# A transformer pair in split fp32: the split weights' slots are shifted against the moving operands

## The chip, the core and the metric

The kernel runs on one core of a Trainium2 chip. The metric is the device time of one execution in microseconds. Three executions of the kernel before took 3043.42, 3047.98 and 3048.37 us; the median is 3047.98 us.

## What is computed

Two layers of one block on 512 tokens of width 1024, then one pass of a second block. Every product with a weight matrix is what matters here:

```python
proj = x @ w_in                                   # 1024 x 2336, twice
h = layer_norm(ALPHA * x + heads @ w_o, g, b)     # attention of three kinds before it
ffn = (silu(h @ w_gate) * (h @ w_up)) @ w_down    # inner width 2816
# second block, once
h  = h  + 0.5 * g1  * swiglu(modulate(h,  ...), w_ffn1_in, w_ffn1_out)
hc = hc + 0.5 * g1c * swiglu(modulate(hc, ...), w_ffn1_in, w_ffn1_out)   # 256 context tokens
q, k, v, rg, cv, ga, gb = split(modulate(h, ...) @ w_in)                 # retention, convolution, gates
h  = h + g2 * ((sigmoid(ga) * y_ret + sigmoid(gb) * y_conv) @ w_out)
h  = h + 0.5 * g3 * swiglu(modulate(h, ...), w_ffn2_in, w_ffn2_out)
out = rmsnorm(h, final_norm)
```

## The kernel before

Activations are held transposed: a tile has 128 features on the partitions and 512 tokens along the row (256 for the context). A weight chunk of 128 output features is one tile of 128 x 1024 fp32, eight slices of 128 columns, one for each 128 input features.

Products are made in three parts. A value is held as a rounded part `hi` (type fp32r) and the rest `lo`. `split` (L106) makes them: ScalarE copies the fp32 tile to `hi` (L108), VectorE subtracts (L109). `mm3` (L139) then issues three matmuls into one PSUM tile: `hi` weights with `hi` data (L141), `hi` weights with `lo` data (L142), `lo` weights with `hi` data (L143). `chunk` (L145) runs `mm3` over the slices. So each matmul has its own load of 128 weight columns, and the data stream past them: 512 columns in the rows named `mm`, 256 in the rows named `gc` and `dc` and in the halves.

`wload` (L111) brings one chunk: a DMA from SyncE's queue to a slot of the pool `wraw` (three slots of 4096 bytes a partition), then `split` into a `hi` and a `lo` slot. These come from the pool `whl`, three slots each, and while a pool `whx` is held (`hold`, L127, two slots each, in three stretches: from each layer's `w_o` to the end of its feed-forward part, and from `w_co` to the end of the kernel) from five in turn. In `vproj` (L1068) the roles are changed: the tokens are the stationary operand and the split weights of `w_v` move.

The order of work is the program's order. Each engine runs its own queue; the tile framework puts in the semaphores, and the scheduling of loads follows from the three raw slots and the three or five split slots.

Where tiles lie: pools are stacked from the left end of a partition in the order in which they are opened, those with `side="right"` from the right end. A tile takes its row's bytes, rounded up to 32. From the left come a reserved stretch, `const` (identity, `ones`, three columns `col128`, `col256`, `col1024`, the pair `blk`, the table `vec`, some small tables), `wraw`, `whl`, `small`, `tmp`, `xp` (the sixteen x tiles of 2048 bytes) and the pools of each stage. From the right come `top` with the tile `pad` of 96 bytes, then the accumulators, the context's tiles and `whx`. Adding up these sizes, the start of every `hi` and `lo` slot, of every x tile, hidden tile, head tile and context tile leaves the same remainder, 384, when it is divided by 512; in the retention stage the tiles of the pool `ret` leave 0, weights and data alike. The slice k of a chunk starts 512 bytes times k further on, so that every weight slice and the data that move past it start at the same remainder. The one exception is `w_kr` (L636), whose slices have 64 columns: every second one starts 256 bytes off.

Of the kernel before, what the change touches and what calls it, by code (L numbers as in the profile page):

```python
# [9 lines left out]
F32 = mybir.dt.float32  # L10
F32R = mybir.dt.float32r
# [51 lines left out]
class Kern:  # L63
    def __init__(self, ctx, tc, a, o):
        self.ctx, self.tc, self.nc, self.a, self.o = ctx, tc, tc.nc, a, o
        pool = lambda name, bufs, **kw: ctx.enter_context(tc.tile_pool(reuse_waits=RW, name=name, bufs=bufs, **kw))
        self.const = pool("const", 1)

        self.nc.vector.memset(pool("top", 1, side="right").tile([128, 24], F32, name="pad"), 0.0)
        self.wraw = pool("wraw", 3)  # L70
        self.whl = pool("whl", 3)
        self.small = pool("small", 2)
        self.tmp = pool("tmp", 2)
        self.xp = pool("xp", 1)
        self.dram = pool("scratch", 1, space=DRAM)
        self.ps_mm = pool("ps_mm", 3, space=PSUM)
        self.ps_s = pool("ps_s", 2, space=PSUM)
        self.ps_t = pool("ps_t", 2, space=PSUM)
        self.ps_o = pool("ps_o", 1, space=PSUM)
        nc = self.nc  # L80
        c = self.const
        self.ident = c.tile([128, 128], F32, name="ident")
        make_identity(nc, self.ident)
        self.ones = c.tile([128, 128], F32, name="ones")
        nc.vector.memset(self.ones, 1.0 / 128)
        self.col = {}
        self.pre = {}
        self.whx = None
        self.turn = 0
        self.nlo = 0  # L90
        for n in (128, 256, 1024):
            t = c.tile([128, 1], F32, name=f"col{n}")
            nc.vector.memset(t, 1.0 / n)
            self.col[n] = t
        self.blk = c.tile([128, 2], F32, name="blk")
        nc.vector.memset(self.blk, 0.0)
        nc.vector.memset(self.blk[0:64, 0:1], 1.0 / 64)
        nc.vector.memset(self.blk[64:128, 1:2], 1.0 / 64)
        self.vec = c.tile([128, NVEC], F32, name="vec")
# [11 lines left out]
    def wload(self, src, key=None):  # L111
        if key in self.pre:
            return self.pre.pop(key)
        n = src.shape[-1]
        raw = self.wraw.tile([128, 1024], F32, tag="raw", name="raw")[:, :n]
        self.nc.sync.dma_start(out=raw, in_=src)
        p = self.whl
        if self.whx is not None:
            if self.turn % (3 + self.nx) >= 3:
                p = self.whx  # L120
            self.turn += 1
        hi = p.tile([128, 1024], F32R, tag="hi", name="whi")[:, :n]
        lo = p.tile([128, 1024], F32R, tag="lo", name="wlo")[:, :n]
        self.split(raw, hi, lo)
        return hi, lo

# [1368 lines left out]
```

## Time and profile before

| what | value |
|---|---|
| runs | 3043.42, 3047.98, 3048.37 us (median 3047.98) |
| profiled execution, its own time | 3048.77 us |
| span of that execution, first to last instruction | 3047.0 us |
| mean granted TensorE clock | 0.996 of full speed |
| TensorE busy / weight loads busy | 3000.2 us (98%) / 2562.3 us (84%) |
| VectorE, ScalarE, GpSimd busy | 1883.5, 1138.7, 141.0 us |

The profile tells for each engine what it ran and what ended its idle time. TensorE's matmuls are pipelined: a row shows one from its start to the arrival of its last result, which overlaps the next one's, so the pace is read from start to start and not from the durations. PEld is the load of weights, which runs beside the matmul before.

### The profile page before, as it was taken

Reading aid. Unit: us, or ns where it says so; the run is one execution under the profiler, and the core shown is the slowest. Engines: PE = TensorE matmul, PEld = TensorE weight load, DVE = VectorE, ACT = ScalarE, POOL = GpSimd, SP = SyncE. Lnnn points to the kernel's source line nnn. Section 1 sums busy time; section 2 is a strip of 40 time slices with the busy share of each in tenths; the row PEclk is TensorE's granted clock in tenths of the full one; section 3 lists DMA queues with packets and bytes.
Section 4 is the critical chain, followed back from the end, with each engine's and each line's share of the span. In section 5 each row is a group of like instructions: output and inputs, shape, how many; then the busy total and the mean of one; then the engine's idle time right before and its main releaser. Section 6 shows DMA issues by size and latency. Waiting matters only on the chain.

```text
span 3047.0 us, 40882 instructions
## 1 busy us (share of the span) xinstructions
PE 3000.2 (98%) x15961; PEld 2562.3 (84%) x15961; DVE 1883.5 (62%) x3649; ACT 1138.7 (37%) x1876; POOL 141.0 (5%) x261
## 2 busy tenths in 40 slices
PE   9999999999999999999999999999999999999998
PEld 6779888887788888888888898988888878888887
DVE  5898757586987554573323338587987766553334
ACT  4764322245755222362121127433233253342222
POOL 0220000000310000000000000000000000000000
PEclk9999999999999999999999999999999999999999
DMA  4452545423443454232212125623323325233332
GB/s 140 108 126 84 182 139 193 130 94 81 117 122 125 154 172 138 90 105 73 73 53 73 56 72 195 205 86 119 101 81 113 118 88 162 87 103 97 97 95 62
DMA packets 109411, 343.53 MB, mean 113 GB/s; under 512 B 14317, under 2 KB 17517, under 8 KB 109089
## 3 DMA queue, kind: packets, MB, share of 16 engines
q1 hardware_dynamic: 89232, 289.83, 30.0%
q0 software_dynamic: 18896, 50.03, 6.1%
q8 instruction: 126, 2.06, 0.3%
q10 hardware_dynamic: 1088, 1.05, 0.1%
q14 instruction: 69, 0.56, 0.1%
HBM read 312.51 MB, written 14.71 MB: 107 GB/s over the span
## 4 chain that ended last, share of the span: by engine, by line
PE 88%; issue 4%; DVE 4%; ACT 2%; DMA 1%; POOL 0%; DVEq 0%; POOLq 0%; ACTq 0%; SPq 0%
PE mm L142 25%; PE mm L141 25%; PE mm L143 25%; PE gc L143 1%; PE gc L142 1%; PE gc L141 1%; PE pvps L370 1%; DVE cz L1136 1%; PE tps L354 1%; ACT P L326 1%; DVE wlo L109 1%; PE dc L143 1%; PE dc L142 1%; PE dc L141 1%; PE sps L141 0%
## 5 line engine op out<-in xcount | busy, mean ns | idle before, releaser
L108 ACT CAST whi<-raw 128x1024 fp32r<-128x1024 f32 (+3 forms) x524 | 506.2, 967 | 1385.8 <-PE mm L142 1192.9
L141 PE MATMUL mm<-uh,whi 128*128 128x512 f32 (+2 forms) x2288 | 860.2, 380 | 6.2 <-DVE uh L264 4.4
L142 PE MATMUL mm<-ul,whi 128*128 128x512 f32 (+2 forms) x2288 | 862.3, 378 | 1.5 <-DVE ul L266 1.2
L143 PE MATMUL mm<-uh,wlo 128*128 128x512 f32 (+2 forms) x2288 | 860.4, 377 | 0.8 <-DVE wlo L109 0.8
L109 DVE TENSOR_TENSOR wlo<-raw,whi 128x1024 fp32r<-128x1024 f32 (+3 forms) x524 | 585.2, 1118 | 415.1 <-ACT whi L108 401.9
L141 PEld LDWEIGHTS mm<-uh,whi 128*128 128x128 f32 (+1 forms) x2288 | 430.1, 189 | 84.4 <-DVE uh L264 5.6
L142 PEld LDWEIGHTS mm<-ul,whi 128*128 128x128 f32 (+1 forms) x2288 | 432.9, 189 | 79.0 <-DVE ul L266 3.4
L143 PEld LDWEIGHTS mm<-uh,wlo 128*128 128x128 f32 (+1 forms) x2288 | 432.6, 189 | 79.0 <-DVE wlo L109 1.6
L141 PE MATMUL mm<-hh,whi 128*128 128x512 f32 (+1 forms) x789 | 289.9, 367 | 1.1 <-DVE acc L975 1.1
L142 PE MATMUL mm<-hl,whi 128*128 128x512 f32 (+1 forms) x789 | 290.4, 368 | 0.0
L143 PE MATMUL mm<-hh,wlo 128*128 128x512 f32 (+1 forms) x789 | 289.5, 367 | 0.3 <-DVE wlo L109 0.3
L516 DVE TENSOR_TENSOR g<-g,mm 128x512 f32<-128x512 f32 (+1 forms) x96 | 61.7, 643 | 270.7 <-PE mm L143 266.0
L1136 DVE SCALAR_TENSOR_TENSOR cz<-cy,vec,cz 128x512 f32<-128x512 f32 x240 | 174.6, 749 | 2.1
L141 PEld LDWEIGHTS mm<-hh,whi 128*128 128x128 f32 x789 | 148.9, 189 | 25.3 <-ACT uch L262 1.5
L143 PEld LDWEIGHTS mm<-hh,wlo 128*128 128x128 f32 x789 | 148.9, 189 | 25.3 <-DVE wlo L109 0.7
L142 PEld LDWEIGHTS mm<-hl,whi 128*128 128x128 f32 x789 | 149.0, 189 | 23.4 <-issue 0.2
L975 DVE SCALAR_TENSOR_TENSOR acc<-mm,g,acc 128x512 f32<-128x512 f32 (+1 forms) x61 | 43.1, 707 | 146.2 <-PE mm L143 146.2
L143 PE MATMUL gc<-uch,wlo 128*128 128x256 f32 x352 | 99.9, 285 | 2.6 <-DVE wlo L109 2.6
L142 PE MATMUL gc<-ucl,whi 128*128 128x256 f32 x352 | 99.8, 284 | 0.0
L141 PE MATMUL gc<-uch,whi 128*128 128x256 f32 x352 | 99.6, 283 | 0.0
L326 ACT ACTIVATE P<-P,nm 128x128 f32<-128x128 f32 (+3 forms) x160 | 88.1, 554 | 14.5 <-DVE nm L322 14.5
L901 DVE CUSTOM_DVE_ANT_0 mr<-mr,srow,vec 128x1024 f32<-128x1024 f32 x72 | 92.1, 1279 | 1.1 <-ACT srow L892 1.1
(387 smaller groups left out, 4790.5 us busy)
## 6 DMA issues: line engine op xcount, KB each, us to landing
mr<-w_mod SPq DMA_DIRECT2D x72, 512.0 KB, 3.9
raw<-w_f1i SPq DMA_DIRECT2D x54, 512.0 KB, 3.5
raw<-w_gate SPq DMA_DIRECT2D x44, 512.0 KB, 3.5
raw<-w_up SPq DMA_DIRECT2D x44, 512.0 KB, 3.5
raw<-w_f2i SPq DMA_DIRECT2D x44, 512.0 KB, 3.5
raw<-w_in SPq DMA_DIRECT2D x36, 512.0 KB, 3.9
raw<-w_v SPq DMA_DIRECT2D x32, 512.0 KB, 4.3
raw<-w_qk SPq DMA_DIRECT2D x24, 512.0 KB, 3.7
```

What stands on the lines that cost most here:

```text
L108: nc.scalar.copy(hi, src)
L109: nc.vector.tensor_tensor(out=lo, in0=src, in1=hi.bitcast(F32), op=ALU.subtract)
L141: mm(out=ps, lhsT=w[0], rhs=x[0], start=first, stop=False)
L142: mm(out=ps, lhsT=w[0], rhs=x[1], start=False, stop=False)
L143: self.last_mm = mm(out=ps, lhsT=w[1], rhs=x[0], start=False, stop=last)
L326: nc.scalar.activation(out=sl, in_=sl, func=AF.Exp, scale=scale, bias=nm[:, qb:qb + 1], accum_out=sm[:, qb:qb + 1])
L354: nc.tensor.transpose(out=ps[:, w:w + 128], in_=Pt[:, OFF[qb] + kb * 128:OFF[qb] + kb * 128 + 128], identity=self.ident)
L370: nc.tensor.matmul(out=out[:, kb * 128:512], lhsT=v, rhs=blocks[kb][part], start=i == 0, stop=i == 7)
L516: gm = nc.vector.tensor_tensor(out=g, in0=g, in1=pu, op=ALU.mult)
L901: nc.vector.tensor_tensor_reduce(out=raw if i == len(rows) - 1 else junk, in0=raw, in1=rows[i], scale=1.0, scalar=self.vec[:, b0 + j:b0 + ...
L975: self.nc.vector.scalar_tensor_tensor(out=h, in0=ps, scalar=g[:, m:m + 1], in1=h, op0=ALU.mult, op1=ALU.add)
L1136: nc.vector.scalar_tensor_tensor(out=z, in0=y[:, t:t + 512], scalar=w, in1=z, op0=ALU.mult, op1=ALU.add)
```

## The change

Every `hi` and `lo` slot grows, by 32 bytes in `whl` and for `hi` in `whx`, by 192 bytes for `lo` in `whx`. Tiles in use are still the first n columns. The three constant columns and `blk` become slices of one tile of 32 bytes, where they took 128; the tile `pad` and its memset go. With that the total of bytes stays: everything between `whl` and the right end starts 96 bytes further on, on the right too.

```diff
-        self.nc.vector.memset(pool("top", 1, side="right").tile([128, 24], F32, name="pad"), 0.0)
...
-        for n in (128, 256, 1024):
-            t = c.tile([128, 1], F32, name=f"col{n}")
-            nc.vector.memset(t, 1.0 / n)
-            self.col[n] = t
-        self.blk = c.tile([128, 2], F32, name="blk")
+        cols = c.tile([128, 8], F32, name="cols")
+        for i, n in enumerate((128, 256, 1024)):
+            self.col[n] = cols[:, i:i + 1]
+            nc.vector.memset(self.col[n], 1.0 / n)
+        self.blk = cols[:, 4:6]
...
-        hi = p.tile([128, 1024], F32R, tag="hi", name="whi")[:, :n]
-        lo = p.tile([128, 1024], F32R, tag="lo", name="wlo")[:, :n]
+        hi = p.tile([128, 1032], F32R, tag="hi", name="whi")[:, :n]
+        lo = p.tile([128, 1032 if p is self.whl else 1072], F32R, tag="lo", name="wlo")[:, :n]
```

Adding up the sizes again: x, hidden, head, accumulator and context tiles now leave 480 when divided by 512. The slots of `whl` start 192, 160 and 128 bytes (`hi`) and 96, 64 and 32 bytes (`lo`) before that place, those of `whx` 448 and 416 (`hi`), 384 and 192 bytes (`lo`) before it. The raw slots, which lie ahead of `whl`, start 96 bytes earlier than they did.

## Rows read from the trace of the kernel before

**Rows 1.** Page: busy time, chain of waits by engine.
```profile
PE 3000.2 (98%) x15961; PEld 2562.3 (84%) x15961; DVE 1883.5 (62%) x3649; ACT 1138.7 (37%) x1876; POOL 141.0 (5%) x261
...
PE 88%; issue 4%; DVE 4%; ACT 2%; DMA 1%; POOL 0%; DVEq 0%; POOLq 0%; ACTq 0%; SPq 0%
```

**Rows 2.** Windows, line L141 alone: window, length, busy (instructions), clock, DMA.
```profile
0.00:3047.00 3047.00, 1742.05 (x4921) 930.55 (x4921) 1.00 0.37 113
```

**Rows 3.** Timeline, a down projection: start us, us, engine, line, instruction, count.
```profile
1000.21 0.39 PE L141 MATMUL mm<-uh,whi 128*128 128x512 f32 x1
...
1005.65 0.39 PE L141 MATMUL mm<-uh,whi 128*128 128x512 f32 x1
```

**Rows 4.** Timeline, TensorE alone, the context's chunk between two chunks of 512 columns.
```profile
1507.45 0.28 PE L141 MATMUL gc<-uch,whi 128*128 128x256 f32 x1
1507.56 0.28 PE L142 MATMUL gc<-ucl,whi 128*128 128x256 f32 x1
1507.68 0.28 PE L143 MATMUL gc<-uch,wlo 128*128 128x256 f32 x1
...
1510.32 0.40 PE L141 MATMUL mm<-uh,whi 128*128 128x512 f32 x1
1510.56 0.40 PE L142 MATMUL mm<-ul,whi 128*128 128x512 f32 x1
```

**Rows 5.** Timeline where TensorE's clock was low, and the same stretch by windows.
```profile
2464.99 0.63 PE L141 MATMUL mm<-uh,whi 128*128 128x512 f32 x1
...
2467.55 0.63 PE L141 MATMUL mm<-uh,whi 128*128 128x512 f32 x1
2464.00:2468.00 4.00, 4.00 (x14) 3.15 (x14) 2.70 (x12) 2.12 (x3) 0.90 (x2) 0.59 0.42 136
```

**Rows 6.** Timeline, matmuls 1845 to 1848 us; then the weight loads there.
```profile
1845.77 0.39 PE L141 MATMUL mm<-hh,whi 128*128 128x512 f32 x1
1846.00 0.39 PE L142 MATMUL mm<-hl,whi 128*128 128x512 f32 x1
1845.77 0.19 PEld L142 LDWEIGHTS mm<-hl,whi 128*128 128x128 f32 x1
1847.41 0.19 PEld L141 LDWEIGHTS mm<-hh,whi 128*128 128x128 f32 x1 [1.45 <-ACT uch L262]
```

**Rows 7.** Groups, 1846.0 to 1846.3 us, shapes apart: count, busy us, mean ns.
```profile
L141 PE MATMUL mm<-hh,whi 128*128 128x512 f32 x1 | 0.4, 390 | 0.0
L142 PE MATMUL mm<-hl,whi 128*128 128x512 f32 x1 | 0.4, 388 | 0.0
```

**Rows 8.** Timeline, TensorE, the chunk of `w_kr` (64 weight columns).
```profile
28.60 0.40 PE L141 MATMUL mm<-xh,whi 128*64 128x512 f32 x1
...
31.36 0.40 PE L141 MATMUL mm<-xh,whi 128*64 128x512 f32 x1
```

**Rows 9.** Timeline, the start of the kernel.
```profile
0.82 0.08 DVE L69 MEMSET pad<- 128x24 f32 x1 [0.82 <-PEq L1487]
...
1.22 0.06 DVE L98 MEMSET blk<- 64x1 f32 x1
...
5.84 1.23 DVE L109 TENSOR_TENSOR wlo<-raw,whi 128x1024 fp32r<-128x1024 f32 x1 [4.56 <-ACT whi L108]
```

**Rows 10.** Groups by shape, the two halves of a split of 1024 columns.
```profile
L108 ACT CAST whi<-raw 128x1024 fp32r<-128x1024 f32 x390 | 409.8, 1051 | 1021.5 <-PE mm L142 875.5 <-issue 112.5 <-PE mm L143 13.9
L109 DVE TENSOR_TENSOR wlo<-raw,whi 128x1024 fp32r<-128x1024 f32 x390 | 476.8, 1223 | 332.4 <-ACT whi L108 319.3 <-PE kps L185 4.2 <-PE mm L143 1.7
```

**Rows 11.** TensorE's waits on `wlo`: us in total, times, longest.
```profile
PE mm L143 <- DVE wlo L109: 3.8, 9, 0.7
PE gc L143 <- DVE wlo L109: 2.6, 2, 1.5
PE mm L142 <- DVE wlo L109: 1.9, 3, 0.9
```

**Rows 12.** DMA issues: count, KB each, median us to landing.
```profile
raw<-w_o SPq DMA_DIRECT2D x16, 512.0 KB, 4.4
...
raw<-w_co SPq DMA_DIRECT2D x8, 512.0 KB, 3.4
```

## The prediction, made before the changed kernel ran

> **What bounds the kernel now.** I read the busy line and the chain first: TensorE is busy for 3000.2 us of the span and carries 88% of the chain; DMA has 1% of it, VectorE 4% [rows 1]. So the end moves when TensorE's pace moves, or its waits. The lines L141 to L143, where split weights meet data, have 4921 matmuls each, 14,763 in all [rows 2]. Durations of pipelined matmuls overlap, so I went on to the timeline for the pace from start to start. A chunk of 24 matmuls of 512 columns takes 1005.65 - 1000.21 = 5.44 us, 226.7 ns each [rows 3]. A chunk of 24 of 256 columns takes 1510.32 - 1507.45 = 2.87 us, 119.6 ns each [rows 4]. The difference, 107.1 ns for 256 columns, is 2.39 columns a ns, the clock's upper level of 2.4 GHz. What is left is the same in both: 226.7 - 213.3 = 13.3 ns and 119.6 - 106.7 = 12.9 ns. Each matmul thus costs its columns and some 13.3 ns, in all 14,763 x 13.3 = 197 us. That sum is the only large thing that the places of weights could act on, and it is what I have to judge.
>
> **The change part by part.**
>
> *The places of the split slots.* Before, weight slices and the data that stream past them start at one remainder of 512 bytes everywhere (worked out from the tile sizes). After, the distances are 32 to 448 bytes. No matmul is added, removed or moved; the numbers of loads and of columns stay. What could change is the 13.3 ns. Three readings bear on it.
>
> First, whether the 13.3 ns come from weights being read beside the stream. The matmul at 1846.00 us has no weight load beside it: its own ran from 1845.77 to 1845.96, the next one starts only at 1847.41 [rows 6]. It lasts 388 ns; the one before it, with a load beside it, 390 ns [rows 7]. If the load took 13.3 ns from the stream, I would expect the first to be that much shorter. It is shorter by 2. Ends of matmuls are modelled in this view, so this is an indication and no proof.
>
> Second, at the lower clock (0.59 in that window) six matmuls of 512 columns take 2467.55 - 2464.99 = 2.56 us, 426.7 ns each, which is 512 columns at 1.2 GHz with nothing left over [rows 5]. The load beside them reads the same bytes. So the extra is not a fixed number of reads that the stream must always give up; it is something that only shows when the array asks for data at full pace.
>
> Third, it isn't quite a constant. The first interval of the context's chunk is 0.11 us, the next 0.12 [rows 4]; where 512 columns follow 256, the first interval is 0.24 us [rows 4], and within a chunk the pace comes back to 226.7. So the pace settles, and something in the order of events sets where.
>
> [...]
>
> I bound this part from both sides by rows. On the gaining side, all 13.3 ns could go: -197 us. If it fell to what the first interval of a context chunk shows, 0.11 instead of 0.12 us, that is some 6.7 ns (half of the 13.3; the row's digits allow 0 to 20): -99 us. On the losing side, the chunk of `w_kr` is the only one where half of the slices lie 256 bytes off the moving place; its 12 intervals take 31.36 - 28.60 = 2.76 us, 230.0 ns each [rows 8], 3.3 more than elsewhere. The matmuls on split slots are 14,763 less those of scores and retention that take no slot, 3 x (96 + 48 + 96) = 720 by the loops, so 14,043: +46 us. I take 0, because the nearest row to the question, a matmul with and without a load beside it, shows no price; both ends stay for the range.
>
> *The splits.* The copy of 1024 columns takes 1051 ns, the subtraction 1223 ns [rows 10]. Nothing in them changes but addresses, all still multiples of 32. TensorE waits 8.3 us in total, 14 times, for `wlo` [rows 11]. If the subtraction became 10% slower or faster, 14 x 0.12 us = 1.7 us would be lost or won; the cover for the rest is TensorE's own work, two to five chunks ahead. I take 0.
>
> *The raw slots 96 bytes earlier.* No row shows a transfer to another remainder. Between loads of the same 512 KB the landing differs from 3.4 to 4.4 us [rows 12], so a quarter up or down is the widest that I allow; on DMA's 1% of the chain, 30 us [rows 1], that is 8 us either way. I take 0: the loads keep their size, count and queue, and everything stays a multiple of 32 bytes.
>
> *Pad and columns.* One memset of 0.08 us on VectorE goes. It runs at 0.82 us; VectorE is done with its constants at 1.28 us and then idles for 4.56 us until ScalarE gives it the first `hi` [rows 9]. So it is worth nothing; without that cover it would be 0.08 us. The columns and `blk` in one tile are written once, before anything reads them; at worst a reader waits for the last of these memsets, at 1.28 us, long done. Nothing is queued behind it.
>
> *Sum.* 0 on a profiled execution of 3048.77 us (span 3047.0 and 1.8 around it). It is 0.8 us above the median of the runs, so I predict that median, 3048.0 us.
>
> **Rivals.**
>
> *Faster: the common place is what costs the 13.3 ns.* Weight load and stream start together, both at 1845.77 us [rows 6], at the same remainder; if they ask for the same part of the memory in step, every distance other than zero would free them. For it: the extra is equal in chunks of 256 and 512 columns, as a price per load would be, and all distances before are zero, so that the trace can't show it absent. Against it: the matmul without a load beside it, and the lower clock with nothing left over. With half of it gone the time is 3048 - 99 = 2949 us; with all of it 2851; with only a tenth, 3028.
>
> *Slower: the settled pace is lost.* The 226.7 ns may be the pace at which loads and streams settle just because they always meet in the same way. With six to ten different distances they need not, and each matmul would cost what `w_kr` costs, 230.0 ns: 3048 + 46 = 3094 us. It decides as soon as the mean interval in a down projection passes 227 ns, everywhere at once. For it: `w_kr` never settles in 24 matmuls, while a chunk of 512 columns after the context does. Against it: `w_kr` also loads half as many columns, which may be the cause by itself.
>
> *Slots are at other places than I added up.* If some pool starts elsewhere, a slot could meet the data at distance zero again; the pace there would be as before, and with all of them 3048 us. This is a part of "no change".
>
> **How the numbers follow.** A measurement of this kernel tells a change from none at about 0.2%, 6 us. No change has 0.62: the direct comparison speaks for it, but all pairs before lie at one distance, so the trace has hardly looked at the others. Slower has 0.20, spread from 6 us to 46 and a little over, as a part of the slots may be hit. Faster has 0.18, spread from 6 to 197 us. The splits and raw slots add at most 10 us to either side and little chance. No change alone lies within 3042 to 3054. To leave out no more than 2 in 10, I go up to 3088, which takes in most of the slower cases (0.16 of 0.20), and down to 3005, which takes in the smaller gains (0.05 of 0.18): 0.62 + 0.16 + 0.05 = 0.83.
>
> **What would show it.** Right: a chunk of 24 matmuls of 512 columns still takes 5.44 us in each stage, one of 256 columns 2.87, and L69 is gone. Faster would show as 215 to 225 ns from start to start, slower as 228 to 232, or as a pace that differs from slot to slot, with periods of three or five chunks. The forecast is wrong if TensorE's pace moves with the slot; were the time to move at an equal pace, the waits on raw tiles or `wlo` must have grown or gone.

## The result, and the profile after

The changed kernel takes 3080.76 us, the median of four runs (3079.74 to 3083.47); the kernel before, run beside it, 3048.16 us. The ratio is 1.0112, with a 95% interval of 1.0095 to 1.013: slower by 33 us. The time lies within the range; the likeliest case, no change, did not happen, and the rival "the settled pace is lost" did.

The page of the changed kernel: busy time, and the chain of waits by engine.

```profile
PE 3032.2 (98%) x15961; PEld 2554.8 (83%) x15961; DVE 1883.7 (61%) x3648; ACT 1139.3 (37%) x1876; POOL 141.0 (5%) x261
...
PE 90%; issue 4%; DVE 2%; ACT 2%; DMA 1%; POOL 1%; DVEq 0%; POOLq 0%; ACTq 0%; SPq 0%
```

The numbers of matmuls and loads are those of [rows 1]; VectorE has one instruction less, the pad's memset. TensorE's busy time grew by 3032.2 - 3000.2 = 32.0 us and the span by 3079.1 - 3047.0 = 32.1 us. All of the loss is in TensorE's own pace, and none in its waits. The lines have moved up by one: L140 to L142 are the three matmuls now. By windows, line L140 alone (columns as in [rows 2]):

```profile
0.00:3079.10 3079.10, 1752.96 (x4921) 924.67 (x4921) 1.00 0.36 112
```

The count and the granted clock are those of [rows 2]. The pace isn't, as the timeline shows (start, duration): a chunk of 24 matmuls of 512 columns in a stage like that of [rows 3], and then the context's chunk that answers to [rows 4].

```profile
1015.78 0.39 PE L140 MATMUL mm<-uh,whi 128*128 128x512 f32 x1
...
1021.35 0.40 PE L140 MATMUL mm<-uh,whi 128*128 128x512 f32 x1
...
1506.91 0.28 PE L140 MATMUL gc<-uch,whi 128*128 128x256 f32 x1
...
1509.74 0.39 PE L140 MATMUL mm<-uh,whi 128*128 128x512 f32 x1
```

24 matmuls of 512 columns take 5.57 us, 232.1 ns each, where it was 226.7. 24 of 256 columns take 2.83 us, 117.9 ns each, where it was 119.6. So the wide matmuls lost 5 ns and the narrow ones won nearly 2. Over all that follow one of their own kind in the trace, from start to start and without those that waited: 512 columns went from 227.18 to 231.98 ns (about 8,720 of them), 256 columns from 119.77 to 118.23 (about 4,770). 8,720 x 4.80 - 4,770 x 1.54 = 41.9 - 7.3 = 34.5 us, close to the 32.1 us of the spans.

What else the prediction priced stayed, as it said. The start (timeline of VectorE), the halves of a split (groups by shape), TensorE's waits on `wlo` (us in total, times, longest) and the landing of loads:

```profile
0.95 0.08 DVE L92 MEMSET cols<- 128x1 f32 x3
...
5.66 1.22 DVE L107 TENSOR_TENSOR wlo<-raw,whi 128x1024 fp32r<-128x1024 f32 x1 [4.40 <-ACT whi L106]
...
L106 ACT CAST whi<-raw 128x1024 fp32r<-128x1024 f32 x390 | 409.1, 1049 | 1057.4 <-PE mm L141 904.1 <-issue 114.2 <-PE mm L142 12.6
L107 DVE TENSOR_TENSOR wlo<-raw,whi 128x1024 fp32r<-128x1024 f32 x390 | 476.2, 1222 | 340.9 <-ACT whi L106 329.4 <-PE kps L184 4.3
...
PE mm L142 <- DVE wlo L107: 3.5, 8, 0.9
PE mm L141 <- DVE wlo L107: 2.9, 3, 1.6
PE gc L142 <- DVE wlo L107: 2.8, 2, 1.5
...
raw<-w_o SPq DMA_DIRECT2D x16, 512.0 KB, 4.6
raw<-w_co SPq DMA_DIRECT2D x8, 512.0 KB, 3.7
```

The first `hi` still comes 4.40 us after VectorE's last constant, so the memset that went was covered ([rows 9]: 4.56). The copies take 1049 ns and the subtractions 1222, against 1051 and 1223 [rows 10]; the waits on `wlo` are 9.2 us, against 8.3 [rows 11]; the loads land 0.2 to 0.3 us later than in [rows 12] and DMA has 1% of the chain as before.

### The profile page after: what moved, and what is told of

Same layout as the page of the kernel before. It is cut to its first block, busy times and chain, and to the rows that moved or that the text cites. A ratio compares the mean times of both kernels' runs of the same rounds, so it can differ in the third digit from the quotient of the medians.

```text
span 3079.1 us, 40881 instructions
## 1 busy us (share of the span) xinstructions
PE 3032.2 (98%) x15961; PEld 2554.8 (83%) x15961; DVE 1883.7 (61%) x3648; ACT 1139.3 (37%) x1876; POOL 141.0 (5%) x261
## 4 chain that ended last, share of the span: by engine, by line
PE 90%; issue 4%; DVE 2%; ACT 2%; DMA 1%; POOL 1%; DVEq 0%; POOLq 0%; ACTq 0%; SPq 0%
PE mm L140 26%; PE mm L141 26%; PE mm L142 26%; PE gc L142 1%; PE gc L141 1%; PE gc L140 1%; PE pvps L369 1%; PE tps L353 1%; PE dc L141 1%; PE dc L142 1%; ACT P L325 1%; PE dc L140 1%; PE sps L140 0%; ACT whi L106 0%; DVE wlo L107 0%
## 5 line engine op out<-in xcount | busy, mean ns | idle before, releaser
L140 PE MATMUL mm<-uh,whi 128*128 128x512 f32 (+2 forms) x2288 | 870.0, 384 | 6.4 <-DVE uh L263 4.4
L141 PE MATMUL mm<-ul,whi 128*128 128x512 f32 (+2 forms) x2288 | 869.4, 381 | 1.5 <-DVE ul L265 1.2
L142 PE MATMUL mm<-uh,wlo 128*128 128x512 f32 (+2 forms) x2288 | 867.3, 380 | 0.8 <-DVE wlo L107 0.8
L142 PEld LDWEIGHTS mm<-uh,wlo 128*128 128x128 f32 (+1 forms) x2288 | 431.9, 189 | 90.7 <-DVE wlo L107 1.6
L140 PEld LDWEIGHTS mm<-uh,whi 128*128 128x128 f32 (+1 forms) x2288 | 429.6, 189 | 91.6 <-DVE uh L263 5.7
L141 PEld LDWEIGHTS mm<-ul,whi 128*128 128x128 f32 (+1 forms) x2288 | 431.8, 189 | 87.5 <-DVE ul L265 3.6
L140 PE MATMUL mm<-hh,whi 128*128 128x512 f32 (+1 forms) x789 | 293.2, 372 | 0.9 <-DVE acc L974 0.9
L141 PE MATMUL mm<-hl,whi 128*128 128x512 f32 (+1 forms) x789 | 292.4, 371 | 0.0
L142 PE MATMUL mm<-hh,wlo 128*128 128x512 f32 (+1 forms) x789 | 291.7, 370 | 0.3 <-DVE wlo L107 0.3
L142 PEld LDWEIGHTS mm<-hh,wlo 128*128 128x128 f32 x789 | 148.6, 188 | 29.1 <-DVE wlo L107 0.7
L140 PEld LDWEIGHTS mm<-hh,whi 128*128 128x128 f32 x789 | 148.4, 188 | 27.1 <-ACT uch L261 1.3
L141 PEld LDWEIGHTS mm<-hl,whi 128*128 128x128 f32 x789 | 148.4, 188 | 26.1 <-issue 0.2
L142 PE MATMUL gc<-uch,wlo 128*128 128x256 f32 x352 | 98.9, 282 | 2.8 <-DVE wlo L107 2.8
L141 PE MATMUL gc<-ucl,whi 128*128 128x256 f32 x352 | 99.5, 283 | 0.0
L140 PE MATMUL gc<-uch,whi 128*128 128x256 f32 x352 | 98.9, 281 | 0.0
```

The lines of the kernel that those rows point to most:

```text
L140: mm(out=ps, lhsT=w[0], rhs=x[0], start=first, stop=False)
L141: mm(out=ps, lhsT=w[0], rhs=x[1], start=False, stop=False)
L142: self.last_mm = mm(out=ps, lhsT=w[1], rhs=x[0], start=False, stop=last)
```

## The experiments

All distances below are the start of a weight slice less the start of the moving operand (the data that stream past it), modulo 512 bytes; the kernel before has 0 everywhere but in `w_kr`. "Ahead" is a weight slice at the higher place, "behind" or "before" at the lower. A stream of matmuls has settled when its interval from start to start, its pace, no longer drifts. Theory A: this distance sets the pace of a matmul. Rivals: B, that the trouble is that `hi` and `lo` slots start at different places; C, that it is not the slots but what else the change did.

**The columns alone.** The columns share a tile, the slots are as before; a pad on the right side keeps all places equal.

```diff
-        hi = p.tile([128, 1032], F32R, tag="hi", name="whi")[:, :n]
-        lo = p.tile([128, 1032 if p is self.whl else 1072], F32R, tag="lo", name="wlo")[:, :n]
+        hi = p.tile([128, 1024], F32R, tag="hi", name="whi")[:, :n]
+        lo = p.tile([128, 1024], F32R, tag="lo", name="wlo")[:, :n]
```

> This does the second part of the change alone: the constant columns share a tile, everything behind them starts 96 bytes earlier, and the tile at the right end takes 192 bytes so that both sides move alike. The split slots keep 4096 bytes, so every weight slice starts at the place of the moving operand again (all leave 288 divided by 512). Theory A (the distance between a weight slice and the operand that moves beside its load sets the pace): 3048 us, chunks of 24 matmuls of 512 columns in 5.44 us. Theory B (the distance doesn't matter, but the loads of one group of three start at different remainders, hi, hi, lo): 3048 us too. Theory C (the columns, or places that are multiples of 32 bytes alone and no longer of 128): 3080 us, chunks of 5.57 us.

Measured: 3046.9 us, ratio 0.9999 (0.999 to 1.0008). 512 columns 227.17 ns, 256 columns 119.76, as before. C falls: what else the change did costs nothing, so the slots make the loss. All places moved by 96 bytes together here, to 288, and it cost nothing; a place by itself is not what counts.

**One distance for all.** Slots of 4096 bytes again, and gaps that put every slot, `hi` and `lo`, 192 bytes before the moving operands.

```diff
+        self.nc.vector.memset(pool("mid", 1).tile([128, 48], F32, name="pad"), 0.0)
...
+        g = st.enter_context(self.tc.tile_pool(reuse_waits=RW, name="gapx", bufs=1, side="right"))
+        g.tile([128, 48], F32, name="gap")
```

> As the changed kernel, but the split slots keep 4096 bytes and 192 bytes lie between them and everything that moves: every hi and lo slot, on both sides, starts 192 bytes before the place of the moving operands (modulo 512), the same for all. Theory A (distance to the moving operand): as the changed kernel, about 3080 us, some 232 ns for 512 columns. Theory B (different starts of hi and lo): as the kernel before, 3048 us and 226.7 ns.

Measured: 3082.29 us, ratio 1.0118 (1.0101 to 1.0135). The timeline: a chunk of 512 columns, then one of 256.

```profile
1003.75 0.39 PE L143 MATMUL mm<-uh,whi 128*128 128x512 f32 x1
...
1009.35 0.39 PE L143 MATMUL mm<-uh,whi 128*128 128x512 f32 x1
...
1506.91 0.28 PE L143 MATMUL gc<-uch,whi 128*128 128x256 f32 x1
...
1509.63 0.39 PE L143 MATMUL mm<-uh,whi 128*128 128x512 f32 x1
```

5.60 us for 24, 233.3 ns each, and 2.72 us, 113.3 ns each: a steady pace again, 6.7 ns above the old one for 512 columns and 6.7 below for 256. `hi` and `lo` lie alike and the loss is there in full. B falls, A holds; and the loss is no matter of irregular places.

**`hi` and `lo` in one tile.** The two parts of a chunk lie at one distance, and each slot at its own: 96, 64 and 32 bytes behind in `whl`, 128 and 64 behind in `whx`.

```diff
+        both = p.tile([128, 2064 if x else 2056], F32R, tag="hl", name="whl")
+        hi, lo = both[:, :n], both[:, 1024:1024 + n]
```

> hi and lo of one chunk lie in one tile, 4096 bytes apart, so that both have the same distance; the slots grow by 32 and 64 bytes, so that the five slots lie 96, 64, 32, 128 and 64 bytes before the moving operands. Theory A: 3075 to 3085 us, and each of the five distances shows in its chunks at 231 to 233 ns for 512 columns; a distance of 128 or 64 may be better. Theory B: 226.7 ns within each chunk whatever its distance, a little lost where one chunk follows another, 3048 to 3053 us.

Measured: 3082.79 us, ratio 1.0116 (1.0101 to 1.0131). Timeline, one chunk on the slot 64 behind, one on the slot 32 behind:

```profile
980.15 0.39 PE L142 MATMUL mm<-uh,whl 128*128 128x512 f32 x1
...
985.65 0.39 PE L142 MATMUL mm<-uh,whl 128*128 128x512 f32 x1
...
991.25 0.40 PE L142 MATMUL mm<-uh,whl 128*128 128x512 f32 x1
...
996.85 0.40 PE L142 MATMUL mm<-uh,whl 128*128 128x512 f32 x1
```

5.50 us (229.2 ns) and 5.60 us (233.3 ns): the pace goes with the slot. The slot 64 behind shows 229 in `whl` (at the left end of the row) and in `whx` (at the right end) alike, so it is not the pool.

**Only `hi` away.** `lo` at distance 0, `hi` 192 bytes before it, so that two matmuls of each three are off.

```diff
+            self.between[id(p)] = p.tile([128, 48], F32, tag="between", name="between", bufs=1)
```

> The lo slots lie at the place of the moving operands, the hi slots 192 bytes before it, on both sides. Theory A: two of the three loads of a group are off, so between half and all of the loss, 3065 to 3080 us. Theory B: the starts of hi and lo differ as in the changed kernel, so 3080 us.

Measured: 3083.36 us, ratio 1.0119 (1.0104 to 1.0134); 512 columns 232.47 ns, 256 columns 118.02. With two of three off the kernel takes as long as with all three, and 3 us more than the 3080 that A had allowed at most; B, which expects 3080 here too, had fallen by the kernel with one distance for all. The 512-column matmuls bear nine tenths of the loss that they have with all three off (233.05 ns). Nor does the price lie on the matmuls that are off. By the place in the group of three the intervals are 231.9 and 232.5 ns for the two on `hi` and 233.6 ns for the one on `lo`, which is itself at distance 0; the second of these runs beside the load of a `lo` slice at 0 (in the trace of the kernel before, the matmul of L142 and the load of L143 both start at 1000.44 us) and is no quicker for it. So a stream with some of its matmuls off settles at a pace of its own.

**The other distances.** Two more kernels with the parts in one tile, some small tables moved behind the slots: `whl` 64, 96 and 128 ahead with `whx` 224 and 160 behind, then `whl` 160, 192 and 224 ahead with `whx` 32 ahead and 256 away. From the first:

```diff
-        self.modv = self.const.tile([128, 72], F32, name="modv")
+        self.modv = self.behind.tile([128, 72], F32, name="modv")
```

> A survey of further distances: a chunk's hi and lo lie in one tile, so that the three slots of the left pool lie 64, 96 and 128 bytes ahead of the moving operands and the two of the right pool 224 and 160 behind them (all modulo 512). Theory A (the distance between a matmul's weights and its moving operand, modulo 512, sets the settled pace): every slot has a pace of its own; the 512-column matmuls lie between 229 and 234 ns, none at the 226.7 of distance 0, and 64 ahead is like 64 behind (229.1 ns in the kernel with hi and lo together); the 256-column ones lie between 113 and 122 ns, lowest near 192 behind (113.3 there). Time by that: about 9,000 matmuls x 4 to 6 ns less some 5,000 x 1 to 3 ns, 3,070 to 3,090 us. Rival B (what counts is whether a slot begins at the common place or not, or in which of the two pools it lies): all slots of a pool show one pace, 231 to 233 ns for 512 columns, whatever the distance.

> The rest of the survey: left slots 160, 192 and 224 bytes ahead of the moving operands, right slots 32 ahead and 256 away. Theory A: 512 columns between 229 and 234 ns, and 256 bytes away like the matmuls of the kernel before with odd slices of 256 bytes, 230.0 ns; 192 ahead need not be like 192 behind (233.3 and 113.3 ns there), since in vproj, where the roles are turned, 192 ahead took 117.9 ns for 256 columns. Time 3,070 to 3,090 us. Rival B: one pace for a pool, whatever the distance.

Measured, one run each: 3093.09 us, 3 above the range that was expected, and 3083.6 us. Rival B of these two falls: the slots of one pool differ. From the second kernel's timeline, chunks on three slots: 192 ahead (first two rows), 32 ahead, then 256 away.

```profile
980.04 0.39 PE L144 MATMUL mm<-uh,whl 128*128 128x512 f32 x1
...
985.54 0.40 PE L144 MATMUL mm<-uh,whl 128*128 128x512 f32 x1
...
996.74 0.39 PE L144 MATMUL mm<-uh,whl 128*128 128x512 f32 x1
...
1002.34 0.39 PE L144 MATMUL mm<-uh,whl 128*128 128x512 f32 x1
...
1007.80 0.39 PE L144 MATMUL mm<-uh,whl 128*128 128x512 f32 x1
```

5.50 us (229.2 ns), 5.60 us (233.3) and 5.46 us (227.5, its first matmuls still in the pace of the slot before). I had expected 230.0 at 256, by `w_kr`, and that was wrong; so was 64 ahead like 64 behind (233.4 against 229.1 in the table below). The paces of the 512-column matmuls whose neighbours lie at the same distance, from start to start, out of the kernels so far (650 matmuls a value or more):

| distance d, bytes | 0 | 32 | 64 | 96 | 128 | 160 | 192 | 224 |
|---|---|---|---|---|---|---|---|---|
| at d, ns | 226.8 | 233.3 | 233.4 | 234.3 | 232.6 | 233.3 | 229.4 | 233.4 |
| at d + 256, ns | 226.9 | 233.4 | 233.3 | 234.5 | 232.8 | 233.3 | 229.1 | 233.4 |

Each pair agrees to 0.3 ns, in different pools and kernels: the pace follows the distance modulo 256 bytes. The changed kernel's 232 ns lie among the paces of its distances (`hi` 64, 96, 128 and `lo` 160, 192, 224 modulo 256 in `whl`); as a mixed stream has a pace of its own, the table gives them no closer than that.

**All slots 256 away, and all 64 behind.** Two tests of this table on whole kernels, with gaps as in the kernel with one distance: 64 words beside `whx` for 256 away (with some small tables moved behind the slots), 16 for 64 behind.

```diff
+        g.tile([128, 64], F32, name="gap")
```

> All slots, hi and lo, in both pools, begin 256 bytes from the moving operands (modulo 512); the columns share a tile. Theory A' (in the survey the right slot at 256 ran its 512-column matmuls at 226.88 ns, and each distance went like the one 256 bytes from it: 229.2 and 229.4 at 64 behind and 192 ahead, 233.3 at 32 ahead and 233.35 at 224 behind; so the pace follows the distance modulo 256): 226.7 ns and 120 ns as before, 3,047 us, ratio 1.000. Rival (modulo 512, by the w_kr matmuls of the kernel before, 230.0 ns where every other slice lies 256 bytes off): about 9,000 x 3.3 ns more, 3,075 us.

> All slots begin 64 bytes before the moving operands. Theory A' with the paces of the survey: 512 columns 229.2 ns against 226.8 (about 9,000 x 2.4 ns = 22 us more), 256 columns 117.6 against 120.5 (about 5,000 x 2.6 ns = 13 us less): 3,056 us, ratio 1.003. Rival (any distance but 0 and 256 costs the same; the survey's 229 came from the slots at other distances around it): 512 columns at 233 ns, 3,080 us.

Timeline of the one 256 away, a chunk of 512 columns:

```profile
1003.78 0.39 PE L145 MATMUL mm<-uh,whi 128*128 128x512 f32 x1
...
1009.22 0.39 PE L145 MATMUL mm<-uh,whi 128*128 128x512 f32 x1
```

Measured 256 away: 3045.18 us, ratio 0.9993 (0.9984 to 1.0003), 5.44 us for the chunk as in [rows 3]; 512 columns 227.17 ns, 256 columns 119.77. Modulo 256 holds and the rival by `w_kr` falls.

The one 64 behind, the same chunk:

```profile
1003.66 0.39 PE L144 MATMUL mm<-uh,whi 128*128 128x512 f32 x1
...
1009.16 0.39 PE L144 MATMUL mm<-uh,whi 128*128 128x512 f32 x1
```

Measured 64 behind: 3049.43 us, ratio 1.0011 (1.0001 to 1.002), where 1.003 was expected; 5.50 us for the chunk, 229.2 ns. Over all, 512 columns took 229.02 ns and 256 columns 117.35, which gives 8,720 x 1.84 - 4,760 x 2.42 = 4.5 us; the medians differ by 2.6. The loss is a difference of two terms of some 10 to 20 us, and I had taken the first too large. The rival, 3,080 us, falls.

**The context apart.** If each matmul's own distance counts, the narrow ones can have theirs: slots and 512-column operands at 0, but `uch`, `ucl` and the context's part of the hidden tiles 192 bytes further on.

```diff
+        self.cp.tile([128, 48], F32, name="gap")
...
+                    self.hid.tile([128, 48], F32, name="gap", bufs=1)
+                hidden[j] += tuple(self.hid.tile([128, 256], F32R, tag=t, name=t) for t in ("ch", "cl"))
```

> The columns share a tile and all slots lie at the moving operands' place, as in the kernel with the columns alone (0.9999 of before), but the moving operands of the context's 256-column matmuls (uch, ucl and the context part of the hidden layer, ch and cl) lie 192 bytes behind every slot's place, so that the weights are 192 bytes before them; the 512-column ones keep distance 0. Theory A (the distance of each matmul's own two operands sets its pace): 512 columns stay at 226.7 ns, the gate-up and down matmuls of the context go from 120 to 113.3 ns, 1,056 (gc) + 528 (dc) + 192 (mm on uch) = 1,776 matmuls x 6.67 ns = 11.8 us less: 3,036 us, ratio 0.996. Rival D (the pace comes from the whole stream: a place that differs from the others disturbs the 512-column matmuls between the context's chunks, or the 113.3 ns came from the 512-column ones being slower): no gain, 3,047 to 3,052 us.

Measured: 3042.51 us, ratio 0.9988 (0.9978 to 0.9997). It beats both kernels, the one before by 5 us with an interval that just leaves out 1, and not by the 12 us expected. Over all, 256 columns took 118.69 ns, and 4,780 x (119.77 - 118.69) = 5.2 us. Timeline: 24 matmuls within the long first stretch of context work, then a chunk between chunks of 512 columns.

```profile
1291.71 0.28 PE L143 MATMUL gc<-uch,wlo 128*128 128x256 f32 x1
...
1294.43 0.28 PE L143 MATMUL gc<-uch,wlo 128*128 128x256 f32 x1
...
1503.78 0.28 PE L141 MATMUL gc<-uch,whi 128*128 128x256 f32 x1
...
1506.61 0.39 PE L141 MATMUL mm<-uh,whi 128*128 128x512 f32 x1
```

113.3 ns in the first, 117.9 in the second, at one distance and in one kernel. Where 512-column matmuls at distance 0 come before, the context's chunk settles at the slower of two paces, in all 48 such chunks of this trace; in the kernel with one distance for all, where 512-column matmuls at distance 64 (modulo 256) come before, it settled at the faster. The 512-column matmuls kept theirs (227.00 ns), so the rival's reason doesn't hold either.

The distance of the work before is not the whole of it. In the kernel with one distance for all, too, the first long stretch of context work has both paces, and four small matmuls between were enough to go from one to the other:

```profile
1328.79 0.28 PE L145 MATMUL gc<-uch,wlo 128*128 128x256 f32 x1
...
1329.69 0.28 PE L144 MATMUL gc<-ucl,whi 128*128 128x256 f32 x1
1329.81 0.60 PE L179 MATMUL rR<-ident,rsy 128*128 128x128 f32 x4
...
1330.37 0.28 PE L143 MATMUL gc<-uch,whi 128*128 128x256 f32 x1
...
1333.20 0.28 PE L143 MATMUL gc<-uch,whi 128*128 128x256 f32 x1
```

Before the small ones eight matmuls take 0.90 us, 113 ns each to the digits of the rows; soon after them 24 take 2.83 us, 117.9 ns each, with every slot 192 behind all the while.

**Other distances for the context.** 32 for the gate and up matmuls with 96 for the down ones, then 224 with 128 (modulo 256); only the widths of the gaps differ.

> The kernel with the context's moving operands apart, at other distances: the weights of the context's gate and up matmuls (gc, and mm on uch) 32 bytes ahead of their moving operand modulo 256, those of its down matmuls (dc) 96 ahead. Those at 64 settled at 117.8 ns where 512-column matmuls of distance 0 ran before them and at 113.3 where 256-column ones or 512-column ones of distance 64 did. Theory E (which of several settled paces a distance takes depends on what ran before): gc and dc here settle anywhere from 113.3 to 122 ns, 3,036 to 3,050 us. Rival (the pace is the distance's alone): gc 117 to 121.5, dc 119, as these distances showed in the surveys, 3,043 to 3,048 us.

> The same with 224 bytes (modulo 256) for gc and mm on uch, 128 for dc. By the surveys' paces alone: gc 116.8 and dc 118.7 ns, 1,248 x 3.2 + 528 x 1.3 = 4.7 us less than with all at distance 0, 3,042 us. Theory E: anywhere from 113.3 to 122 ns, 3,036 to 3,048 us.

Measured, one run each: 3044.82 and 3044.24 us. The context's chunks of 24 gate and up matmuls took 118.3 and 116.8 ns each, those of 18 down matmuls 118.9 and 119.8, against 119.7 and 119.6 in the kernel before. Three of the four lie near what these distances showed in the surveys; the last, expected at 118.7, is 1.1 ns off, and nothing near 113.3 appeared. So at these distances the two runs don't settle theory E against its rival; at 64 the two paces above have. They show that between chunks of 512 columns at distance 0 no distance tried for the context gains more than 119.7 - 116.8 = 2.9 ns a matmul.

## Why the prediction was right in its range and wrong in its likeliest case

- **The sum of 13.3 ns a matmul as the only large thing** held: the loss is in the pace of these matmuls and nowhere else. It comes on top of the 13.3 ns, though, and for 256 columns takes some away. The 13.3 itself is an estimate: 226.7 less half of the 426.7 ns that 512 columns take where the granted clock is 0.50 (windows of the kernel before, 2465.00 to 2467.50 us; the 0.59 of [rows 5] is the mean of a longer stretch). The prediction's 2.4 GHz and 1.2 GHz stand for columns a ns: 2.39 at a granted clock of 1.00 [rows 3, 4], 512 / 426.7 = 1.20 at 0.50. No run shows a frequency.
- **The places of the split slots: "I take 0, because the nearest row to the question, a matmul with and without a load beside it, shows no price."** This step failed. 388 against 390 ns [rows 7] compares a load with no load at distance 0, and so says nothing of what a load at another distance does to the stream; besides, they are durations with modelled ends, not a pace. The row that looked at another distance, `w_kr` with its 230.0 ns [rows 8], had been set aside for its half loads. By its price the loss would be 46 us; between the spans it is 32.1. What the runs showed in place of the 0: 512 columns went from 227.18 to 231.98 ns and 256 columns from 119.77 to 118.23, and the distance, modulo 256 bytes, is what moved them.
- **The rival "the settled pace is lost"** named the right place, the right sign and the right sight: 228 to 232 ns, and a pace that differs from slot to slot. Two things in it were off. The pace isn't lost, it settles elsewhere: at one distance for all it is as steady as before, at 233.3. And its anchor was right by luck: slots 256 away cost nothing (512 columns took 227.17 ns), so the 256 bytes as such can't be the cause of the 230.0 ns of `w_kr`. The loads of half as many columns are left, or the change between 0 and 256 from slice to slice; no run tells them apart.
- **What I did not foresee**: the 256-column matmuls gain, 1.54 ns on average, and give back 7.3 us. The prediction had one price for both widths.
- **The bounds.** The gaining side, up to 197 us, rested on all 13.3 ns falling away. For 512 columns none of the sixteen distances came below the 226.8 of distance 0; for 256 columns half of it went: 113.3 is some 6.7 ns above 106.7, which is an estimate, a quarter of the 426.7 ns of 512 columns at half the clock [rows 5]. That is the size that the prediction had taken from the first interval in [rows 4]; the digits of that row allowed 0 to 20 ns, so the match is luck.
- **The low clock as a sign** that the extra shows only at full pace [rows 5] holds at the one other distance shown here. In the second survey kernel the slot at distance 224 has these rows in the timeline, and the window its clock (0.50):

```profile
205.12 0.63 PE L144 MATMUL mm<-xh,whl 128*128 128x512 f32 x1
...
208.54 0.63 PE L146 MATMUL mm<-xh,whl 128*128 128x512 f32 x1
204.00:208.00 4.00, 4.00 (x11) 3.14 (x10) 4.00 (x10) 1.36 (x2) 2.02 (x3) 0.50 0.86 224
```

  Eight matmuls in 3.42 us, 427.5 ns each: the 426.7 of distance 0 to the digits of the rows. In these rows, at a granted clock of 0.50, the distance costs nothing; over whole runs, whose mean granted clock is 0.99, the same distance costs 233.4 - 226.8 = 6.6 ns.
- **Splits, raw slots, pad and columns** at nothing were right, by the rows above and by the kernel with the columns alone.

Where the weight slice and the moving operand begin, one against the other, changed the pace of 512 columns from 226.8 to as much as 234.5 ns, so in this kernel the distance is not free, though the prediction took 0 for it.

## What to carry to other kernels

Where every matmul has its own weight load, as in this kernel, look up the starts of weight slices and moving operands modulo 256 bytes before resizing any tile near them: 32 to 192 bytes more a slot moved this kernel by 1% (ratio 1.0112). If all starts share one remainder, the trace can't price another; a kernel with slots at several distances, like the two of the survey here, read from start to start and never by durations, prices several in one run. And price each width by itself: of the distances tried, what is best for 512 columns (0, with 226.8 ns) is not what is best for 256 (64, with 113.3 ns in the faster of its two paces, against 119.77 at 0).

## What the runs showed of the hardware that I had not expected

- The pace of fp32r matmuls with a load each follows the distance between weights and moving operand modulo 256 bytes: 226.8 ns at 0, 229.1 to 229.4 at 192, 232.6 to 234.5 at the six others, for 512 columns (mean granted clock of these runs 0.993 to 0.997).
- At distance 64, 256 columns have two settled paces, 113.3 and 117.8 ns, and what ran just before changes which one holds. Which work leads to which is known only for chunks between chunks of 512 columns. Why is not settled, and no run shows what makes the paces repeat after 256 bytes.
- Two matmuls of three at another distance cost nearly as much as all three (232.47 and 233.05 ns over all 512-column ones, against 227.18), and the third, at distance 0, is no quicker than they are (233.6 against 231.9 and 232.5).
